# Lookahead of the weight pipeline in a fused transformer block: sums, casts and residues queued five, four and three units ahead, and the last pass begun with a pair

## The chip, the cores and the metric

The kernel runs on one core of one Trainium2 chip. The metric is device time in microseconds: the median of the runs of a kernel. The kernel before took 1093.7 us (three runs, 1092.52 to 1096.44). One execution more was taken with the hardware profiler; all views of the trace come from it.

## The reference

One layer of a hybrid block on x of 256 tokens by 2048 channels, in float32. The change touches only the last line of it, the SwiGLU part (D = 2048, hidden width 5632).

```python
xn = rms_norm(x, norm1_g)
q, k, v, ga, gg = split(xn @ w_in)          # 2048 -> 5120
att  = differential attention of 4 heads with RoPE, block-causal
u    = conformer convolution of ga * sigmoid(gg)
h    = x + concat(att, u) @ w_out           # 2048 -> 2048
hn   = rms_norm(h, norm2_g)
y    = h + (silu(hn @ w_gate) * (hn @ w_up)) @ w_down   # 2048 -> 5632 -> 2048
```

## The kernel before

**Arithmetic.** Each float32 operand is used as a rounded part (hi, type fp32r) and a residue (lo). A product is three matmuls: hi by hi, lo by hi, hi by lo. So each weight tile that is loaded must be cast on ACT (hi) and its residue must be made before TensorE (PE) can finish with it. The residue is made in one of two ways: DVE subtracts hi from the raw tile, or ACT writes the negated raw tile into lo and the POOL queue starts a DMA that adds the rounded weight's source on top (`by_dma`; these units have capital letters in the orders below).

**Units.** The program is a list of chunks, and PE takes them in this order. The early stages (w_in, w_out, and the first hidden block of gate and up, j = 0) use plain chunks. After that come "units" of two kinds:
- a *two* (letters g, G, u, U): 512 KB of weights, one tile `raw`, hi in `whi`, residue in `wlo`, 12 matmuls.
- a *pair* (letter s): 1 MB of weights in `wb`, on which one step of a Strassen-like scheme with seven products is done. DVE first makes four sums of the weights in `wt` (L963 to L965, three instructions), ACT casts the weights (L966) and the sums (L967) into `wh`, and DVE makes the residues `wl` of both (L971, L972). PE then does 21 matmuls (L988 to L990): for each of the seven products two with `wh` and one with `wl`. The first three products use columns of `wl` that L972 writes.

The stages of units are: gate and up blocks j = 1 to 3, then two passes of w_down (called d0.0 and d0.1), blocks 4 to 7, passes d1.0 and d1.1, blocks 8 to 10, passes d2.0 and d2.1. A block has 4 pairs and 8 twos in the order `sgGsgGsUUsUu` (`gugusgsUsGsU` for j = 1). The passes of w_down have 3 pairs and 10 twos, in the last group 3 pairs and 6 twos. A block needs 180 matmuls, a pass 183, a pass of the last group 135.

**End of a block.** After the last pair of a block DVE folds seven of the eight PSUM banks of products (`bank_sums`, L1086 to L1092), ACT applies SiLU (L1098), after the last unit DVE makes the hidden values (L1106, L1108, called u operations below), PE transposes them (L862) and ACT and DVE make hi and lo forms for w_down (`transposed`, `pair_forms`). These steps are Python generators: each `yield` is one resume, and `resume()` is called four times in a pair and twice in a two, so where a step is queued depends on how many resumes it has waited (`lag`). Passes of w_down add to the output by DMA. For j = 0 the hidden values are made at L829 (`up_done`).

**What sets the order of the work.** Each engine runs its own queue strictly in the order in which the program emits instructions; the order across engines is set by semaphores alone. `run_chunks` (L400) writes the queues: before it emits unit t to PE, it emits loads until unit t+5 (SP queue), casts of `by_dma` units until t+5 (ACT and POOL), the other casts until t+3, and residues until t+2. The sums of a pair are a part of its cast step (`round_pair`, L956), so they too are queued three units ahead. The buffers: 4 of `raw`, 4 of `whi`, 4 of `wlo`, 2 each of `wb`, `wh` and `wl`, 1 of `wt`. A load waits for the tile that it overwrites, whatever its place in the queue.

Of the kernel before, what the change touches and what calls it, by code (L numbers as in the profile page):

```python
# [12 lines left out]
F32 = mybir.dt.float32  # L13
F32R = mybir.dt.float32r
# [4 lines left out]
P = 128  # L19
# [12 lines left out]
N = 512  # L32
# [20 lines left out]
XPARTS = (range(0, 2), range(2, 4), range(4, 8), range(8, 12), range(12, 16))  # L53
# [3 lines left out]
AHEAD = 2  # L57
RAW_BUFS = 4
# [10 lines left out]
FGROUPS = (4, 4, 3)  # L69
# [12 lines left out]

PRODUCTS = ((Q6, 5, 1), (Q7, 6, 2), (Q5, 4, 3), (Q1, 0, 5), (Q2, 1, 6), (Q4, 2, 0), (Q3, 3, 4))

DOWN = (dict(pairs=((1, 0), (1, 1), (2, 0)), order="gsGgsGgsuUuUu"),
        dict(pairs=((4, 0), (4, 1), (5, 0)), order="gsGgsGgsuUuUu"),
        dict(pairs=((8, 0), (8, 1), (9, 0)), order="gsGsgsuUu"))

LOAD_AHEAD, DMA_AHEAD, HI_AHEAD, LO_AHEAD = 5, 5, 3, 2


BLOCKS = 2 * KD + 1
# [1 line left out]
TO_TRANSPOSE = 5  # L94
# [13 lines left out]
def tile_block(  # L108
# [6 lines left out]
    act, dve, pool, pe, sp = nc.scalar, nc.vector, nc.gpsimd, nc.tensor, nc.sync  # L115
# [174 lines left out]
    chunks = []  # L290
# [106 lines left out]
        if c["done"]:  # L397
            start(c["done"](ps))

    def run_chunks():  # L400
        n = len(chunks)
        loaded = split = 0
        rounded = [0, 0]

        def load(i):
            if i in before:
                before[i]()
            chunks[i]["load"](chunks[i])

        def do_round(which, until):  # L410
            while rounded[which] < min(n, until):
                c = chunks[rounded[which]]
                if c["by_dma"] == bool(which):
                    c["round"](c)
                rounded[which] += 1

        for t in range(n):
            load_lead, dma_lead, hi_lead, lo_lead = lead(t)
            while split < min(rounded[0], t + 1 + lo_lead):
                chunks[split]["split"](chunks[split])  # L420
                split += 1
            while loaded < min(n, t + 1 + load_lead):
                load(loaded)
                loaded += 1
                if load_lead == lo_lead:
                    do_round(1, loaded)
                    do_round(0, loaded)
                    chunks[split]["split"](chunks[split])
                    split += 1
            do_round(1, t + 1 + dma_lead)  # L430
            do_round(0, t + 1 + hi_lead)
            while split < min(n, t + 1 + lo_lead):
                chunks[split]["split"](chunks[split])
                split += 1
            chunks[t]["multiply"](chunks[t])
            if chunks[t].get("prompt") and chunks[t]["done"]:
                resume()
        while running:
            resume()
# [373 lines left out]
    ffn = {}  # L813
# [18 lines left out]
        yield from transposed(j, aa)  # L832

    def group_of(j):
        return next(g for g in range(len(FGROUPS)) if j < sum(FGROUPS[: g + 1]))

    def place(g):

        pairs = DOWN[g]["pairs"]
        at = 7 * len(pairs)  # L840
# [10 lines left out]
    def transposed(j, aa):  # L851
        g = group_of(j)
        if g not in down:
            place(g)
        d = down[g]
        for t in range(N // P // 2):
            pool_, tag = (aux_ps, "aux") if j else (acc_ps, "acc")
            pt = pool_.tile([P, 2, S], F32, tag=tag, name="ps_a")
            for i in range(2):
                for m in range(NM):  # L860
                    c = (2 * t + i) * P
                    pe.transpose(pt[:, i, m * P : (m + 1) * P], aa[m][:, c : c + P], ident)  # L862
            if (j, t) in d["pairs"]:
                yield from pair_forms(j, t, pt)
            else:
                hi, lo = d["at"][j, t]
                act.copy(hi, pt)
                yield from lag(2)
                dve.tensor_tensor(lo, pt, hi.bitcast(F32), ALU.subtract)  # L869
            d["ready"].add((j, t))  # L870
            yield from lag(2 if j else 1)

    def pair_forms(j, t, pt):

        fp = ffn["pool"]
        q = down[group_of(j)]["pairs"].index((j, t))
        fhi, flo = (f[:, :, q] for f in down[group_of(j)]["forms"])
        a = fp.tile([P, 2, NM, P], F32, tag="sum0", name="af")
        act.copy(a, pt)
        a11, a21, a12, a22 = a[:, 0, 0], a[:, 0, 1], a[:, 1, 0], a[:, 1, 1]  # L880
        act.copy(fhi[:, :2], a[:, :, 0])
        act.activation(fhi[:, 2], a22, AF.Copy, scale=-1.0)
        yield
        f = fp.tile([P, 4, P], F32, tag="sum2" if j else "sum1", name="fs")
        dve.scalar_tensor_tensor(f[:, 1], a21, -1.0, a22, ALU.mult, ALU.subtract)
        dve.scalar_tensor_tensor(f[:, 2], f[:, 1], -1.0, a11, ALU.mult, ALU.subtract)
        dve.tensor_tensor(f[:, 3], a11, a21, ALU.subtract)
        dve.tensor_tensor(f[:, 0], a12, f[:, 2], ALU.subtract)
        act.copy(fhi[:, 3:], f)
        yield  # L890
        dve.tensor_tensor(flo[:, :2], a[:, :, 0], fhi[:, :2].bitcast(F32), ALU.subtract)
        dve.scalar_tensor_tensor(flo[:, 2], a22, -1.0, fhi[:, 2].bitcast(F32), ALU.mult, ALU.subtract)
        yield
        dve.tensor_tensor(flo[:, 3:], f, fhi[:, 3:].bitcast(F32), ALU.subtract)

    forms = {}
# [56 lines left out]
        src = weights([(w, k, col, N) for w, col in c["sides"] for k in c["ks"]])  # L953
        sp.dma_start(out=c["b"].rearrange("p k n -> p (k n)"), in_=src)

    def round_pair(c):  # L956

        fp = ffn["pool"]
        assert "hi" in forms
        b = c["b"]  # L960
        c["t"] = t = fp.tile([P, 4, N], F32, tag="wt", name="wt")
        c["hi"] = fp.tile([P, 7, N], F32R, tag="wh", name="wh", bufs=2)
        dve.tensor_tensor(t[:, 2:4], b[:, 1:3], b[:, 0:1].to_broadcast([P, 2, N]), ALU.subtract)  # L963
        dve.tensor_tensor(t[:, 1], b[:, 1], t[:, 3], ALU.add)  # L964
        dve.tensor_tensor(t[:, 0], t[:, 1], b[:, 3], ALU.subtract)  # L965
        act.copy(c["hi"][:, 4:], b[:, 1:])  # L966
        act.copy(c["hi"][:, :4], t)  # L967

    def split_pair(c):
        c["lo"] = ffn["pool"].tile([P, 7, N], F32R, tag="wl", name="wl", bufs=2)  # L970
# [94 lines left out]
    def down_block(g, n):  # L1065

        last = g == len(FGROUPS) - 1 and n == D // N - 2
        ks = lambda jt: (jt[0] * (N // P) + 2 * jt[1], jt[0] * (N // P) + 2 * jt[1] + 1)
        pairs = DOWN[g]["pairs"]
        twos = [(j, t) for j in range(sum(FGROUPS[:g]), sum(FGROUPS[: g + 1])) for t in range(2) if (j, t) not in pairs]  # L1070
        units = fast_block(DOWN[g]["order"], ("w_down", n * N), ("w_down", (n + 1) * N),
                           [(q, ks(jt)) for q, jt in enumerate(pairs)], [(jt, ks(jt)) for jt in twos],
                           ready=lambda c: g in down and (pairs[c["p"]] if c["kind"] == "s" else c["p"]) in down[g]["ready"],
                           forms=lambda: down[g]["forms"],
                           plain=lambda c: [tuple(t[:, i, :] for t in down[g]["at"][c["p"]]) for i in range(2)])
# [25 lines left out]
    def block_done(j, q):  # L1101
        while "g" not in halfway:
            yield
        g, u = halfway.pop("g"), halfway.pop("u")
        for m, i in enumerate((Q3, QX)):
            dve.tensor_tensor(u[m], q[i], u[m], ALU.add)  # L1106
        for m in range(NM):
            dve.tensor_tensor(u[m], u[m], g[m], ALU.mult)  # L1108
        yield from lag(TO_TRANSPOSE)
        yield from transposed(j, u)  # L1110

    def add_to_out(m, n, t):
# [58 lines left out]
    for g, nb in enumerate(FGROUPS):  # L1171
# [7 lines left out]
        for n in range(0, D // N, 2):  # L1179
            down_block(g, n)  # L1180
        j0 += nb

    lead = lambda t: ((1,) * 4 if t < len(XPARTS) else (LOAD_AHEAD, DMA_AHEAD, HI_AHEAD, LO_AHEAD)
                      if "kind" in chunks[t] else (AHEAD,) * 4)
    for c, part in enumerate(XPARTS):
        before[c] = lambda part=part: x_load(part)
    before[0] = lambda: (x_load(XPARTS[0]), gain_columns(), x_part(XPARTS[0]), warm_up(WARM[1]), start(x_rest()))
    before[len(XPARTS)] = lambda: start(late_constants())
    run_chunks()


# [32 lines left out]
```

## Time and profile before

| | |
|---|---|
| runs, median (lowest to highest) | 1093.7 us (1092.52 to 1096.44) |
| profiled execution, its time | 1095.98 us |
| its span, first to last instruction | 1094.2 us |
| mean granted TensorE clock | 0.988 |
| DVE, ACT, POOL busy | 902.5, 654.9, 130.5 us |

The views are read like this. The page gives the busy time of each engine over the span. The view of waits lists who waited for whom: the waiting engine with the tile and the line, the releaser, then microseconds in total, how many times, and the longest. The view by windows gives, for each stretch, its length, then busy time (and number of instructions) of PE, of the weight loads PEld, of DVE, ACT and POOL, then the granted clock, the share of the DMA engines and GB/s. The timeline gives start and duration of each instruction, and in square brackets the idle time of the engine before it with what ended it. L and a number is a line of the kernel before.

### The profile page before, as it was taken

What the parts mean: (1) busy time and instruction counts of PE and PEld (TensorE: products, weight loads), DVE (VectorE), ACT (ScalarE), POOL (GpSimd) and SP (SyncE); (2) the same over time, 40 slices, a digit from 0 to 9 for tenths busy, and PEclk for the clock granted to TensorE, in tenths of its full rate; (3) what the DMA queues carried; (4) which work ended last, traced back from release to release, by engine and by line L of the source; (5) the groups of instructions that cost most, each with busy time, mean ns of one, the idle gap of its engine ahead of it and who ended that gap; (6) DMA issues with size and microseconds to landing.
All of it is one profiled execution on the core that took longest, in us unless ns stands there. A gap on an engine that the chain in (4) does not pass through costs nothing.

```text
span 1094.2 us, 13181 instructions
## 1 busy us (share of the span) xinstructions
PE 1051.0 (96%) x4780; PEld 865.5 (79%) x4780; DVE 902.5 (82%) x1124; ACT 654.9 (60%) x831; POOL 130.5 (12%) x176
## 2 busy tenths in 40 slices
PE   8999999999999999989999999899999999899698
PEld 7988888877888877777878888778878888687586
DVE  4799989898755788888878878889796888897877
ACT  6544566755754656657556566576665475766432
POOL 0120112201000000101011211010101110001011
PEclk9999999999999999999999999999999999999899
DMA  8556555444467469798779997978969998888564
GB/s 295 196 183 201 191 175 174 154 154 154 135 212 241 163 232 292 216 277 211 235 227 280 304 316 211 266 208 255 303 172 295 291 280 282 223 260 229 198 180 102
DMA packets 62445, 245.47 MB, mean 224 GB/s; under 512 B 6964, under 2 KB 8430, under 8 KB 54956
## 3 DMA queue, kind: packets, MB, share of 16 engines
q1 hardware_dynamic: 48576, 200.56, 51.6%
q0 software_dynamic: 13744, 44.05, 22.0%
q8 instruction: 37, 0.61, 0.2%
q14 instruction: 28, 0.23, 0.1%
q10 hardware_dynamic: 60, 0.03, 0.0%
HBM read 236.22 MB, written 8.39 MB: 224 GB/s over the span
## 4 chain that ended last, share of the span: by engine, by line
PE 34%; DVE 16%; ACT 8%; issue 6%; DMA 2%; POOL 0%; SPq 0%; DVEq 0%; ACTq 0%
PE q L1007 7%; PE q L1006 7%; PE q L1011 6%; PE q L990 5%; PE q L988 5%; PE q L989 5%; DVE wl L972 4%; ACT wh L967 3%; DMA raw<-in_wts_dram 2%; DVE wt L963 2%; ACT whi L333 2%; DVE wlo L342 2%; ACT wlo L336 2%; DVE wl L971 1%; DVE wt L964 1%
## 5 line engine op out<-in xcount | busy, mean ns | idle before, releaser
L333 ACT CAST whi<-raw 128x1024 fp32r<-128x1024 f32 (+1 forms) x261 | 268.8, 1047 | 134.6 <-DMA raw<-in_wts_dram 54.7
L342 DVE TENSOR_TENSOR wlo<-raw,whi 128x1024 fp32r<-128x1024 f32 (+1 forms) x193 | 233.4, 1218 | 74.6 <-ACT whi L333 74.4
L372 PE MATMUL acc<-whi,lhi 128*128 128x512 f32 (+1 forms) x448 | 168.3, 380 | 3.2 <-ACT lhi L239 2.9
L967 ACT CAST wh<-wt 128x2048 fp32r<-128x2048 f32 x58 | 110.8, 1910 | 99.3 <-DVE wt L965 99.1
L373 PE MATMUL acc<-whi,llo 128*128 128x512 f32 (+1 forms) x448 | 166.5, 376 | 0.5 <-DVE llo L240 0.4
L972 DVE TENSOR_TENSOR wl<-wt,wh 128x2048 fp32r<-128x2048 f32 x58 | 132.9, 2291 | 10.4 <-ACT wh L967 9.6
L990 PE MATMUL q<-wl,fhi 128*128 128x512 f32 x280 | 112.8, 403 | 17.6 <-DVE wl L972 17.6
L337 POOL DMA_DIRECT2D wlo<-in_wts_dram x68 | 61.4, 903 | 553.1 <-ACT wlo L336 468.1
L1006 PE MATMUL q<-whi,chi 128*128 128x512 f32 x320 | 124.7, 390 | 0.0
L1007 PE MATMUL q<-whi,clo 128*128 128x512 f32 x320 | 124.6, 389 | 0.0
L971 DVE TENSOR_TENSOR wl<-wb,wh 128x1536 fp32r<-128x1536 f32 x58 | 101.7, 1753 | 22.2 <-ACT wh L966 22.2
L378 PE MATMUL acc<-wlo,lhi 128*128 128x512 f32 (+1 forms) x448 | 114.4, 380 | 1.7 <-DVE wlo L342 1.7
L988 PE MATMUL q<-wh,fhi 128*128 128x512 f32 x280 | 112.4, 401 | 2.5 <-DVE llo L869 2.4
L989 PE MATMUL q<-wh,flo 128*128 128x512 f32 x280 | 111.5, 398 | 0.0
L526 DVE SCALAR_TENSOR_TENSOR y<-upad,cw,y 128x256 f32<-128x256 f32 x240 | 103.8, 483 | 4.4 <-ACT y L519 3.9
L372 PEld LDWEIGHTS acc<-whi,lhi 128*128 128x128 f32 x448 | 84.9, 189 | 18.9 <-ACT lhi L239 3.3
L373 PEld LDWEIGHTS acc<-whi,llo 128*128 128x128 f32 x448 | 84.9, 190 | 15.7 <-DVE llo L240 0.9
L378 PEld LDWEIGHTS acc<-wlo,lhi 128*128 128x128 f32 x448 | 79.6, 188 | 17.3 <-DVE wlo L342 3.0
L966 ACT CAST wh<-wb 128x1536 fp32r<-128x1536 f32 x58 | 85.1, 1468 | 3.9 <-issue 2.5
L1011 PE MATMUL q<-wlo,chi 128*128 128x512 f32 x320 | 86.4, 392 | 0.0
L990 PEld LDWEIGHTS q<-wl,fhi 128*128 128x128 f32 x280 | 53.9, 192 | 32.6 <-DVE wl L972 21.0
L336 ACT ACTIVATE wlo<-raw 128x1024 fp32r<-128x1024 f32 x68 | 71.7, 1054 | 0.0
(213 smaller groups left out, 1717.6 us busy)
## 6 DMA issues: line engine op xcount, KB each, us to landing
raw<-in_wts_dram SPq DMA_DIRECT2D x259, 512.0 KB, 4.9
wb<-in_wts_dram SPq DMA_DIRECT2D x58, 1024.0 KB, 6.7
wlo<-in_wts_dram POOLq DMA_DIRECT2D x68, 512.0 KB, 8.1
out_dram<-sum POOLq DMA_DIRECT2D x22, 256.0 KB, 7.4
out_dram<-h POOLq DMA_DIRECT2D x8, 256.0 KB, 5.7
h<-in_x_dram SPq DMA_DIRECT2D x6, 256.0 KB, 8.1
h<-in_x_dram SPq DMA_DIRECT2D x4, 128.0 KB, 3.4
raw<-in_wts_dram SPq DMA_DIRECT2D x2, 256.0 KB, 4.3
```

The source lines that it names most:

```text
L333: act.copy(c["hi"], c["raw"])
L342: dve.tensor_tensor(c["lo"], c["raw"], c["hi"].bitcast(F32), ALU.subtract)
L372: pe.matmul(ps[m], xhi[:, ms], hi[:, j, :], start=c["first"] and j == 0, stop=False)
L373: pe.matmul(ps[m], xlo[:, ms], hi[:, j, :], start=False, stop=False)
L378: pe.matmul(ps[m], xhi[:, ms], lo[:, j, :], start=False, stop=c["last"] and j == nk - 1)
L972: dve.tensor_tensor(c["lo"][:, :4], c["t"], c["hi"][:, :4].bitcast(F32), ALU.subtract)
L988: pe.matmul(ps, fhi[:, f, p, :], c["hi"][:, w], start=bool(first), stop=False)
L989: pe.matmul(ps, flo[:, f, p, :], c["hi"][:, w], start=False, stop=False)
L990: pe.matmul(ps, fhi[:, f, p, :], c["lo"][:, w], start=False, stop=bool(last))
L1006: pe.matmul(ps, plain[i][0][:, ms], hi[:, i, :], start=i == 0 and bool(c["first"].get(qs[m])), stop=False)
L1007: pe.matmul(ps, plain[i][1][:, ms], hi[:, i, :], start=False, stop=False)
L1011: pe.matmul(sum_bank(c, qs[m]), plain[i][0][:, ms], lo[:, i, :], start=False, stop=i == 1 and bool(c["last"].get(qs[m])))
```

## The change

The order of the queues for the units is rewritten. The core of the diff:

```diff
-DOWN = (dict(pairs=((1, 0), (1, 1), (2, 0)), order="gsGgsGgsuUuUu"),
-        dict(pairs=((4, 0), (4, 1), (5, 0)), order="gsGgsGgsuUuUu"),
-        dict(pairs=((8, 0), (8, 1), (9, 0)), order="gsGsgsuUu"))
-
-LOAD_AHEAD, DMA_AHEAD, HI_AHEAD, LO_AHEAD = 5, 5, 3, 2
+DOWN = (dict(pairs=((1, 0), (1, 1), (2, 0)), order=("gsGgsGgsuUuUu",) * 2),
+        dict(pairs=((4, 0), (4, 1), (5, 0)), order=("gsGgsGgsuUuUu",) * 2),
+        dict(pairs=((8, 0), (8, 1), (9, 0)), order=("sgsGgsuUu",) * 2))
+
+LOAD_AHEAD, DMA_AHEAD, SUMS_AHEAD, HI_AHEAD, LO_AHEAD = 9, 5, 5, 4, 3
...
+    def may_load(i):
+        c = chunks[i]
+        if "kind" not in c:
+            return False
+        if "sides" in c:
+            o = earlier(pair_at, i, 2)
+            return "hi" in forms and (o is None or o in parted)
+        o = earlier(two_at, i, RAW_BUFS)
+        return o is None or o in parted or (o in rounded and chunks[o]["by_dma"])
...
+    def may_sum(i):
+        o = earlier(pair_at, i, 1)
+        return "sides" not in chunks[i] or (loaded[0] > i and (o is None or o in parted))
...
         for t in range(n):
...
+            if t >= first - AHEAD:
+                until("part", part_of, t + 1 + LO_AHEAD)
+                until("sums", sums_of, t + 1 + SUMS_AHEAD, may=may_sum)
+                until("dma", round_of, t + 1 + DMA_AHEAD, lambda c: c["by_dma"])
+                until("round", round_of, t + 1 + HI_AHEAD)
+                load_until(t + 1 + LOAD_AHEAD)
+            else:
+                until("part", part_of, t + 1 + (1 if t < len(XPARTS) else AHEAD))
+            part_of(t)
             chunks[t]["multiply"](chunks[t])
...
@@ def transposed
-                yield from lag(2)
+                yield from lag(3 if j else 2)
@@ def pair_forms, twice
-        yield
+        yield from lag(2)
...
-    def round_pair(c):
+    def pair_sums(c):
         b = c["b"]
-        c["t"] = t = fp.tile([P, 4, N], F32, tag="wt", name="wt")
+        c["t"] = t = ffn["pool"].tile([P, 4, N], F32, tag="wt", name="wt")
         dve.tensor_tensor(t[:, 2:4], b[:, 1:3], b[:, 0:1].to_broadcast([P, 2, N]), ALU.subtract)
         dve.tensor_tensor(t[:, 1], b[:, 1], t[:, 3], ALU.add)
         dve.tensor_tensor(t[:, 0], t[:, 1], b[:, 3], ALU.subtract)
-        act.copy(c["hi"][:, 4:], b[:, 1:])
-        act.copy(c["hi"][:, :4], t)
+
+    def round_pair(c):
+        c["hi"] = ffn["pool"].tile([P, 7, N], F32R, tag="wh", name="wh", bufs=2)
+        act.copy(c["hi"][:, 4:], c["b"][:, 1:])
+        act.copy(c["hi"][:, :4], c["t"])
...
@@ def block_done
-        yield from lag(TO_TRANSPOSE)
+        yield from lag(TO_TRANSPOSE if group_of(j) == group_of(j + 1) else 3)
```

So residues go from two to three units ahead, casts from three to four, and the sums of a pair, now a step of their own, from three to five, as soon as the pair is loaded and the residues of the pair before it are queued. Loads are queued up to nine units ahead as soon as the instruction that frees their tile is queued. The new rule starts two chunks before the first unit, where the old one kept two chunks of lead. Both passes of the last group begin with a pair instead of a two. After the last block of a group the transposes are queued after three resumes instead of five; the lo forms of a transposed tile come one resume later, the second and third step of the pair forms one each. No instruction is added to or taken from any engine; the number of buffers is the same.

More of the change, by code (lines that the diff above doesn't have):

```diff
@@ L1 @@
+import bisect
 import math
@@ L398, in multiply, with earlier, load_until @@
             start(c["done"](ps))
[L400 to L405, printed above, removed]
+    loaded, rounded, parted = [0], set(), set()
+    pair_at, two_at = [], []
+    def earlier(at, i, n):
+        k = bisect.bisect_left(at, i) - n
+        return at[k] if k >= 0 else None
+    def may_load(i):
[7 more added lines that the diff above has]
+        return o is None or o in parted or (o in rounded and chunks[o]["by_dma"])
+    def load_until(n, forced=False):
+        while loaded[0] < min(n, len(chunks)):
+            i = loaded[0]
+            if not (forced or may_load(i)):
+                return
+            loaded[0] += 1
             if i in before:
@@ L408, in load @@
             chunks[i]["load"](chunks[i])
[L410 to L415, printed above, removed]
-        for t in range(n):
[L418 to L434, printed above, removed]
+    def may_sum(i):
+        o = earlier(pair_at, i, 1)
+        return "sides" not in chunks[i] or (loaded[0] > i and (o is None or o in parted))
@@ new lines, in sums_of, with round_of, part_of @@
+    def sums_of(i):
+        c = chunks[i]
+        if "sides" in c and "t" not in c:
+            load_until(i + 1, True)
+            o = earlier(pair_at, i, 1)
+            if o is not None:
+                part_of(o)
+            pair_sums(c)
+    def round_of(i):
+        if i not in rounded:
+            rounded.add(i)
+            load_until(i + 1, True)
+            sums_of(i)
+            chunks[i]["round"](chunks[i])
+    def part_of(i):
+        if i not in parted:
+            parted.add(i)
+            round_of(i)
+            chunks[i]["split"](chunks[i])
@@ new lines, in run_chunks, with until @@
+    def run_chunks():
+        n = len(chunks)
+        pair_at.extend(i for i, c in enumerate(chunks) if "sides" in c)
+        two_at.extend(i for i, c in enumerate(chunks) if "kind" in c and "sides" not in c)
+        at = dict(part=0, dma=0, sums=0, round=0)
+        first = next(i for i, c in enumerate(chunks) if "kind" in c)
+        def until(what, do, stop, only=lambda c: True, may=lambda i: True):
+            while at[what] < min(n, stop) and may(at[what]):
+                if only(chunks[at[what]]):
+                    do(at[what])
+                at[what] += 1
+        for t in range(n):
+            if t >= first - AHEAD:
[7 more added lines that the diff above has]
+            part_of(t)
@@ L834, in group_of @@
     def group_of(j):
-        return next(g for g in range(len(FGROUPS)) if j < sum(FGROUPS[: g + 1]))
+        return next((g for g in range(len(FGROUPS)) if j < sum(FGROUPS[: g + 1])), None)
     def place(g):
@@ L889, in pair_forms @@
         act.copy(fhi[:, 3:], f)
-        yield
+        yield from lag(2)
         dve.tensor_tensor(flo[:, :2], a[:, :, 0], fhi[:, :2].bitcast(F32), ALU.subtract)
@@ L954, in load_pair @@
         sp.dma_start(out=c["b"].rearrange("p k n -> p (k n)"), in_=src)
-    def round_pair(c):
-        fp = ffn["pool"]
+    def pair_sums(c):
         assert "hi" in forms
         b = c["b"]
-        c["t"] = t = fp.tile([P, 4, N], F32, tag="wt", name="wt")
-        c["hi"] = fp.tile([P, 7, N], F32R, tag="wh", name="wh", bufs=2)
+        c["t"] = t = ffn["pool"].tile([P, 4, N], F32, tag="wt", name="wt")
         dve.tensor_tensor(t[:, 2:4], b[:, 1:3], b[:, 0:1].to_broadcast([P, 2, N]), ALU.subtract)
@@ L1070, in down_block @@
         twos = [(j, t) for j in range(sum(FGROUPS[:g]), sum(FGROUPS[: g + 1])) for t in range(2) if (j, t) not in pairs]
-        units = fast_block(DOWN[g]["order"], ("w_down", n * N), ("w_down", (n + 1) * N),
+        units = fast_block(DOWN[g]["order"][n // 2], ("w_down", n * N), ("w_down", (n + 1) * N),
                            [(q, ks(jt)) for q, jt in enumerate(pairs)], [(jt, ks(jt)) for jt in twos],
@@ L1181, in tile_block @@
         j0 += nb
-    lead = lambda t: ((1,) * 4 if t < len(XPARTS) else (LOAD_AHEAD, DMA_AHEAD, HI_AHEAD, LO_AHEAD)
-                      if "kind" in chunks[t] else (AHEAD,) * 4)
     for c, part in enumerate(XPARTS):
```

## Prediction

> **What bounds the kernel now.** I read the page first, then the waits of PE, then the windows stage by stage.
>
> ```profile
> PE 1051.0 (96%) x4780; PEld 865.5 (79%) x4780; DVE 902.5 (82%) x1124; ACT 654.9 (60%) x831; POOL 130.5 (12%) x176
> PE q L990 <- DVE wl L972: 18.6, 11, 3.5
> PE q L1007 <- DVE llo L869: 4.4, 1, 4.4
> PE q L1006 <- ACT lhi L867: 3.3, 1, 3.3
> PE q L988 <- DVE llo L869: 2.4, 1, 2.4
> PE ps_a L862 <- DVE alo L869: 2.3, 2, 1.2
> ```
>
> PE is the bound, and what it waits for is residues: eleven times those of a pair (L972), and four times a form of the hidden values. Nothing here waits for a load. The windows below run from the first matmul of a stage of units to that of the next (starts from the timeline of PE), in this order: blocks 1, 2, 3, passes d0.0, d0.1, blocks 5, 6, 7, pass d1.0, blocks 9, 10, passes d2.0, d2.1.
>
> ```profile
> 399.07:445.16 46.09, 43.66 (x190) 35.63 (x188) 41.13 (x36) 28.80 (x24) 3.54 (x4) 0.96 0.89 297
> 445.16:492.45 47.29, 42.65 (x189) 34.34 (x188) 42.28 (x53) 30.25 (x32) 4.30 (x5) 1.00 0.81 242
> 492.45:538.53 46.08, 43.71 (x189) 35.64 (x188) 37.52 (x43) 30.29 (x31) 4.34 (x5) 0.96 0.79 218
> 538.53:582.39 43.86, 42.67 (x192) 35.05 (x191) 34.86 (x35) 23.57 (x22) 5.23 (x6) 1.00 0.83 246
> 582.39:623.90 41.51, 41.51 (x185) 34.27 (x183) 35.21 (x33) 26.79 (x24) 7.02 (x8) 1.00 1.00 285
> 664.70:710.78 46.08, 42.39 (x190) 34.41 (x188) 40.86 (x50) 30.05 (x31) 4.30 (x5) 1.00 0.81 231
> 710.78:757.11 46.33, 43.67 (x189) 35.56 (x188) 40.80 (x45) 30.61 (x31) 4.32 (x5) 0.96 0.83 247
> 757.11:798.88 41.77, 41.77 (x190) 34.57 (x188) 34.68 (x35) 27.82 (x26) 4.33 (x5) 1.00 0.84 240
> 798.88:842.64 43.76, 42.65 (x193) 35.06 (x191) 34.77 (x35) 23.47 (x22) 5.21 (x6) 1.00 0.84 247
> 924.96:972.22 47.26, 43.75 (x190) 35.58 (x188) 42.33 (x51) 31.96 (x34) 4.32 (x5) 0.96 0.80 234
> 972.22:1015.09 42.87, 42.06 (x189) 34.49 (x188) 34.95 (x41) 27.64 (x28) 4.35 (x5) 1.00 0.77 209
> 1015.09:1058.15 43.06, 34.83 (x144) 27.63 (x143) 33.40 (x33) 18.60 (x18) 3.47 (x4) 0.88 0.63 183
> 1058.15:1090.05 31.90, 31.39 (x136) 24.92 (x134) 26.80 (x28) 12.04 (x10) 5.14 (x6) 1.00 0.59 149
> ```
>
> Block 7 and pass d0.1 are undisturbed (PE busy throughout at full clock): 41.77 us for 180 matmuls and eight transposes, 41.51 us for 183 matmuls, so 0.227 us a matmul and 41.77 - 180 x 0.227 = 0.9 us for the transposes. A pass with eight transposes should take 42.4, one of the last group 135 x 0.227 = 30.6, with transposes 31.5. What each stage took beyond that is what any schedule could win: block 1 4.3, block 2 5.5, block 3 4.3, d0.0 1.4, blocks 5 and 6 4.3 and 4.6, d1.0 1.3, blocks 9 and 10 5.5 and 1.1, d2.0 11.5, d2.1 1.3. The sum is 45.1 us, about 31 of it waits and the rest the granted clock (0.96 and 0.88) after them. The early stages aren't touched by the change. Something within 0.5% (5.5 us) can't be told from no change here.
>
> **Why the third pair of a block is late.** The timeline of DVE, then of ACT, in block 5:
>
> ```profile
> 681.24 0.69 DVE L965 TENSOR_TENSOR wt<-wt,wb 128x512 f32<-128x512 f32 x1
> 685.21 0.29 DVE L885 SCALAR_TENSOR_TENSOR fs<-af 128x128 f32<-128x128 f32 x1 [3.28 <-ACT af L879]
> 686.69 1.75 DVE L971 TENSOR_TENSOR wl<-wb,wh 128x1536 fp32r<-128x1536 f32 x1
> 688.36 2.28 DVE L972 TENSOR_TENSOR wl<-wt,wh 128x2048 fp32r<-128x2048 f32 x1
> ```
> ```profile
> 682.80 1.91 ACT L967 CAST wh<-wt 128x2048 fp32r<-128x2048 f32 x1
> 684.61 0.58 ACT L879 COPY af<-ps_a 128x512 f32<-128x512 f32 x1
> ACT wh L967 <- DVE wt L965: 99.1, 35, 6.8
> ```
>
> DVE ends the sums at 681.9, stands 3.3 us before the pair forms of block 4, which ACT has queued behind the cast of this pair, and makes the residues only then. Sums, cast and residue of one pair follow each other with no slack, two or three units before PE needs them; ACT waited for such sums 35 times.
>
> **Residues, casts and sums a unit or two earlier.** At the start of a block the new DVE queue reads: sums of the second pair, bank_sums, u operations, residue of the second pair, sums of the third, first pair forms, residue of the third. Counted from the first matmul of the block: bank_sums (4.65 us, rows below) can start when PE ends the last pair, 5.4 us before; the u operations must wait for zero and take 2.56; residue 1.75 + 2.28, a two's residue 1.22, sums 1.22 + 0.69 + 0.69, forms about 1, and the residue of the third pair ends about 16 to 17 us, while PE reaches that pair after 2 x 4.76 + 4 x 2.72 + 0.5 = 21 us. The margin is 4 us where today it is -3.5, and the cast no longer waits for the sums. So I take the pair waits of blocks 2, 3, 5, 6, 9, 10 and d2.1 away, with the clock behind them. What is late next is DVE itself: 40.86 us of work in block 5 against 41.77 of PE. Margins of 1 us will be cut now and then; I leave 1.5 us for all of them. The ends: 0, and half of today's 26.6 us in these stages.
>
> ```profile
> 1010.37 0.68 DVE L1086 COPY sum<-q 128x512 f32<-128x512 f32 x1
> 1014.34 0.68 DVE L1092 TENSOR_TENSOR sum<-q,sum 128x512 f32<-128x512 f32 x1
> 1020.01 1.28 DVE L1108 TENSOR_TENSOR sum<-sum,sum 128x512 f32<-128x512 f32 x2
> ```
>
> **Starts of the passes.** With three resumes the transposes of the last block are queued 18 matmuls (4.1 us) into the pass. In d0.0 and d1.0 DVE has bank_sums, 2.60 of sums and 2.56 of u operations (two groups like L1108) until then and is done at about 5 us: a wait of about 1 us each, in place of 1.4 and 1.3. In d2.0 a pair's residue lies before the u operations: 1015.02 + 4.03 + 2.56 = 1021.6 against 1019.2, a wait of 2.4 plus about 1 of clock. The forms of block 10 then have two pairs and a two of PE's time before the first unit that needs them, so the two waits of 3.3 and 4.4 us of today go. d2.0 loses 3.4 instead of 11.5.
>
> **Block 1 gets worse.** Here the new rule starts before the first unit, and the sums of the first pair come into the DVE queue ahead of a two's residue and ahead of L829, the hidden values of block 0.
>
> ```profile
> 399.51 1.22 DVE L342 TENSOR_TENSOR wlo<-raw,whi 128x1024 fp32r<-128x1024 f32 x1 [0.41 <-ACT whi L333]
> 400.65 1.40 DVE L829 SCALAR_TENSOR_TENSOR a<-acc,rstd,sil 128x512 f32<-128x512 f32 x2
> 402.31 1.48 ACT L966 CAST wh<-wb 128x1536 fp32r<-128x1536 f32 x1 [1.35 <-DMA wb<-in_wts_dram]
> 403.61 0.60 PE L862 MATMUL ps_a<-ident,a 128*128 128x128 f32 x4
> 415.55 0.50 PE L988 MATMUL q<-wh,fhi 128*128 128x512 f32 x1 [2.43 <-DVE llo L869]
> ```
>
> The weights of that pair land at 402.3, and the order of loads and what frees their tiles up to there stay as they are. So DVE, free at 400.7, waits until 402.3, makes the sums (404.9), the residue of the two (406.1) and L829 (407.5). PE wants the transposes at 403.6: a new wait of 3.9 us. Then L869 of block 0, for whose PSUM bank PE waits today 2.43 us in the fourth product of the first pair: DVE has before it residue (4.03), sums (2.60), two's residue (1.22), L869 (0.69), residue of the second pair (4.03), sums of the third (2.60), and itself: 407.5 + 15.9 = 423.4. PE, 3.9 us later than today, is there at 413.1 + 3.9 = 417.0. A wait of about 6 us (the instructions overlap by some tenths). With the clock, 1.9 us today (4.3 less 2.43), block 1 loses 3.9 + 6 + 1.9 = 11.8 in place of 4.3. The ends: 4.3 if the sums wait for nothing, and 13.7 with a second loss of clock.
>
> [...]
>
> **Loads.** The queue of SP keeps its order, and it waits for tiles already, not for its place:
>
> ```profile
> SPq L954 <- DVE wl L971: 327.0, 47, 17.5
> ACT whi L333 <- PE q L1007: 48.1, 18, 6.4
> DMA to landing us min/median/max: 5.2/8.1/11.8
> ```
>
> So nine instead of five is worth nothing by itself; loads start earlier only by as much as the residues free tiles earlier. DMA has the room: share 1.00 in d0.1 with no loss.
>
> **The sum.** 45.1 less what stays (11.8 block 1, 2.0 for d0.0 and d1.0, 3.4 for d2.0, 1.5 others) is 26.4 us. The profiled execution took 1095.98 (span 1094.2), so it would be 1069.6; against the median of the runs, 2.3 lower, 1067.3. I predict 1067.
>
> **Rivals.**
> - *Block 1 doesn't pay* (0.12): the sums wait for no load, or the other waits leave less than I think. Block 1 at 4.3 or below and the rest as above: 1060 to 1054. Against it: the 1.35 us that ACT waits for that very load.
> - *The casts run into their four buffers* (0.12). In the five twos at the end of a pass the cast four units ahead needs a fifth `whi`, so ACT stands until PE is done, with the next pass's pair cast behind it (row L333: 48.1 us of such waits today, where they harm nobody). After 1.8 of the third of these twos ACT needs 1.05 + 1.05 for the two in front, 1.48 + 1.91 for the pair, DVE 2.28: 7.8 us against 9.1 of PE, a margin of 1.3. If the ring makes it wait for the next unit the margin is -1.4; with clock 3 us in four passes: 1079.
> - *Slower* (0.05): DVE comes late to bank_sums. More of its work for coming pairs is queued before them, and the next block's first products need those banks. It decides from 3.8 us late on (5.2 of lead less the 1.4 of two folds). Late by a pair's sums and residue (6.6), each of 15 starts would lose 2.8 and up to 1.9 of clock, 42 to 70 us, against 33 saved: 1102 to 1131. Against it: 40.86 of 41.77 is the fullest block, most have 35.
> - *Accumulates get late, no change* (0.04). A residue made by DMA is started 5 units (13.6 us) before PE's unit, and its second half comes 1.8 us later; less 2.1 on ACT and 0.9 on POOL it may land in 12.4 us. Today's slowest takes 11.8. If more loads in flight made the typical 8.1 into 13, half of the 68 such units would lose 0.6 to 0.8: 1067 + 24 = 1091. [...]
>
> **How the numbers follow.** The forecast has 0.67, 1060 to 1074. The range takes in the first two rivals: 1056 to 1080. Faster by over 0.5%: forecast, first and second rival, 0.91, less a little for worse mixtures: 0.89. Within: 0.06. Slower: 0.05.
>
> **What would show it.** Right: PE's wait for L972 falls from 18.6 to under 4 us; ACT's wait for L965 from 99 to under 30; the windows of blocks 2, 3, 5, 6, 9 come to 42 to 43 us; d2.0 to about 35; PE stands at L862 in block 1 for about 4 us with L829 late, then about 6 us at L988 for L869; block 1 takes 53 to 54. Wrong: pair waits that only move to another pair; new waits of PE for `wlo` landed by DMA or for bank_sums; a short block 1.

## The result and the profile after

The changed kernel takes 1076.5 us (median of four runs, 1075.8 to 1077.3) against 1093.4 for the kernel before in the same series: ratio 0.984, 95% interval 0.982 to 0.986. Run again beside the later experiments it took 1075.1 (ratio 0.981, 0.980 to 0.983). So it is faster by 17 to 20 us, where 26.4 were forecast. The profiled execution took 1075.79 us (span 1074.0).

The lines have new numbers: the residues L971 and L972 are now L1015 and L1016, the sums' last L965 is L1006, the cast L967 is L1011, the transposes L862 are L905, the first matmul of a product L988 is L1032, the forms L867 and L869 are L910 and L912, the first pair form L885 is L928, block 0's hidden values L829 are L872, the folds L1086 to L1092 are L1130 to L1136, the u operations L1106 and L1108 are L1150 and L1152.

First the page's line of busy times, then the waits of PE (engine, tile and line, releaser, us in total, times, longest):

```profile
PE 1044.6 (97%) x4780; PEld 861.5 (80%) x4780; DVE 900.4 (84%) x1124; ACT 654.0 (61%) x831; POOL 129.9 (12%) x176
```
```profile
PE ps_a L905 <- DVE a L872: 4.7, 2, 4.4
PE q L1032 <- DVE llo L912: 4.5, 1, 4.5
PE ps_a L905 <- DVE sum L1152: 4.2, 6, 2.5
...
PE q L1032 <- DVE sum L1130: 1.7, 2, 1.3
...
PE q L1050 <- DVE sum L1135: 1.2, 2, 0.6
...
PE q L1032 <- DVE sum L1134: 0.7, 2, 0.4
```

The waits for the residues of pairs, 18.6 us before, are gone altogether. In their place stand waits for steps of the hidden values: L872, L912, L1152 and the folds (the last three rows, 3.6 us in all).

The windows of the stages (length, PE, PEld, DVE, ACT, POOL busy, granted clock, DMA share, GB/s): blocks 1, 2, 3, pass d0.0, d0.1; blocks 5, 6; block 9; pass d2.0.

```profile
397.04:453.15 56.11, 46.59 (x189) 37.28 (x188) 43.93 (x39) 30.99 (x26) 3.55 (x4) 0.91 0.78 245
453.15:497.16 44.01, 42.39 (x188) 34.31 (x189) 40.09 (x49) 28.08 (x30) 4.31 (x5) 1.00 0.83 248
497.16:540.48 43.32, 42.36 (x189) 34.31 (x189) 39.53 (x45) 28.83 (x29) 4.35 (x5) 1.00 0.89 275
540.48:584.27 43.79, 43.05 (x192) 35.08 (x192) 33.71 (x35) 26.52 (x26) 5.24 (x6) 1.00 0.74 213
584.27:625.75 41.48, 41.48 (x185) 34.35 (x183) 35.76 (x34) 23.91 (x20) 7.04 (x8) 1.00 0.98 278
...
666.55:708.32 41.77, 41.77 (x190) 34.58 (x189) 37.45 (x44) 29.94 (x31) 4.31 (x5) 1.00 0.83 246
708.32:750.43 42.11, 42.09 (x190) 34.49 (x188) 40.62 (x46) 28.83 (x28) 4.33 (x5) 1.00 0.90 277
...
919.03:960.79 41.76, 41.76 (x189) 34.58 (x188) 37.09 (x43) 29.39 (x31) 4.32 (x5) 1.00 0.83 242
...
1002.85:1039.19 36.34, 33.59 (x144) 27.22 (x143) 34.52 (x35) 20.80 (x19) 3.52 (x4) 0.95 0.66 201
```

Blocks 5 and 9 now take the undisturbed 41.77 us. Block 1 has become the worst stage: 56.11 us, where it was 46.09. Some of DVE's operations at the start of block 1 and PE's two long waits there (timelines; start, duration, and in brackets the idle time before):

```profile
401.57 1.23 DVE L1004 TENSOR_TENSOR wt<-wb 128x1024 f32<-128x1024 f32 x1 [2.73 <-DMA wb<-in_wts_dram]
...
405.30 1.40 DVE L872 SCALAR_TENSOR_TENSOR a<-acc,rstd,sil 128x512 f32<-128x512 f32 x2
...
421.52 0.68 DVE L912 TENSOR_TENSOR llo<-ps_a,lhi 128x512 fp32r<-128x512 f32 x1
```
```profile
406.10 0.33 PE L905 MATMUL ps_a<-ident,a 128*128 128x128 f32 x1 [4.36 <-DVE a L872]
...
422.25 0.79 PE L1032 MATMUL q<-wh,fhi 128*128 128x512 f32 x1 [4.45 <-DVE llo L912]
```

DVE stands 2.73 us for the load of the first pair with L872 queued behind the sums, as the prediction read it; PE then stands 4.36 us, and later 4.45 us for L912, which is behind two pairs' residues and sums.

### The profile page after: what moved, and what is told of

Read it like the earlier page. It is cut to its first block, busy times and chain, and to the rows that moved or that the text cites. A ratio compares the mean times of both kernels' runs of the same rounds, so it can differ in the third digit from the quotient of the medians.

```text
span 1074.0 us, 13249 instructions
## 1 busy us (share of the span) xinstructions
PE 1044.6 (97%) x4780; PEld 861.5 (80%) x4780; DVE 900.4 (84%) x1124; ACT 654.0 (61%) x831; POOL 129.9 (12%) x176
## 4 chain that ended last, share of the span: by engine, by line
PE 55%; DVE 7%; issue 2%; ACT 1%; DMA 1%; DVEq 0%; SPq 0%; ACTq 0%
PE q L1050 10%; PE q L1051 10%; PE q L1055 10%; PE q L1032 8%; PE q L1033 8%; PE q L1034 8%; DVE wl L1016 1%; DVE wlo L343 1%; PE ps_a L905 1%; DVE wt L1004 1%; DMA wb<-in_wts_dram 1%; DVE wt L1005 0%; ACT whi L334 0%; DVE wl L1015 0%; ACT wh L1011 0%
## 5 line engine op out<-in xcount | busy, mean ns | idle before, releaser
L1015 DVE TENSOR_TENSOR wl<-wb,wh 128x1536 fp32r<-128x1536 f32 x58 | 101.7, 1753 | 42.5 <-ACT wh L1010 42.5
L1016 DVE TENSOR_TENSOR wl<-wt,wh 128x2048 fp32r<-128x2048 f32 x58 | 132.7, 2287 | 1.0
L1011 ACT CAST wh<-wt 128x2048 fp32r<-128x2048 f32 x58 | 110.8, 1910 | 35.3 <-DVE wt L1006 35.0
L1032 PE MATMUL q<-wh,fhi 128*128 128x512 f32 x280 | 110.8, 396 | 6.8 <-DVE llo L912 4.5
L1034 PE MATMUL q<-wl,fhi 128*128 128x512 f32 x280 | 109.9, 392 | 0.0
L1004 DVE TENSOR_TENSOR wt<-wb 128x1024 f32<-128x1024 f32 x58 | 70.8, 1221 | 4.2 <-DMA wb<-in_wts_dram 3.6
L337 ACT ACTIVATE wlo<-raw 128x1024 fp32r<-128x1024 f32 x68 | 71.8, 1056 | 0.2 <-PE q L1055 0.2
```

The lines of the kernel that those rows point to most:

```text
L1016: dve.tensor_tensor(c["lo"][:, :4], c["t"], c["hi"][:, :4].bitcast(F32), ALU.subtract)
L1032: pe.matmul(ps, fhi[:, f, p, :], c["hi"][:, w], start=bool(first), stop=False)
L1034: pe.matmul(ps, fhi[:, f, p, :], c["lo"][:, w], start=False, stop=bool(last))
```

## The experiments

All are the changed kernel with one or two edits. The table puts their results together. A loss is the time of a stage (from its first matmul to that of the next, by PE's timeline; the last pass to the end of its last unit) beyond the undisturbed length given in the prediction (40.8 us for blocks 4 and 8, which begin without transposes). A wait in front of a stage's first matmul is thus counted to the stage before it. The losses come from one profiled execution of each kernel, the ratios from four to ten runs. "Leads" are the units by which sums, casts and residues are ahead.

| kernel | leads | block 1 | blocks 2 to 10 | d0.0, d1.0 | last group | sum | ratio to before (95%) |
|---|---|---|---|---|---|---|---|
| before | 3/3/2 | 4.3 | 25.3 | 2.7 | 12.7 | 45.0 | 1 |
| changed | 5/4/3 | 14.3 | 5.1 | 2.6 | 4.8 | 26.8 | 0.984 (0.982 to 0.986) |
| changed, again | 5/4/3 | 13.2 | 4.9 | 2.6 | 4.8 | 25.5 | 0.981 (0.980 to 0.983) |
| e1 hold block 1's start | 5/4/3 | 4.9 | 6.1 | 2.6 | 5.9 | 19.5 | 0.974 (0.972 to 0.976) |
| e5 five resumes | 5/4/3 | 12.3 | 5.2 | 1.0 | 3.8 | 22.3 | 0.979 (0.977 to 0.981) |
| e6 old last order | 5/4/3 | 11.9 | 9.1 | 2.6 | 7.3 | 30.9 | 0.990 (0.986 to 0.993) |
| e3 sums alone ahead | 5/3/2 | 7.7 | 31.8 | 7.8 | 2.4 | 49.7 | 1.003 (1.002 to 1.005) |
| e4 sums at four | 4/4/3 | 8.7 | 3.0 | 1.8 | 6.0 | 19.5 | 0.974 (0.973 to 0.976) |
| e10 residues at two | 5/4/2 | 8.2 | 5.7 | 6.2 | 1.0 | 21.1 | 0.979 (0.977 to 0.982) |
| e9 sums four, residues two | 4/4/2 | 7.6 | 1.7 | 0.0 | 0.1 | 9.4 | 0.969 (0.966 to 0.971) |
| e12 all at three | 3/3/3 | 10.0 | 9.5 | 2.0 | 10.7 | 32.2 | 0.985 (0.982 to 0.989) |
| e13 old leads | 3/3/2 | 4.0 | 4.8 | 7.1 | 2.9 | 18.8 | 0.975 (0.971 to 0.979) |
| e8 hold, sums four | 4/4/3 | 4.9 | 3.2 | 1.8 | 6.3 | 16.2 | 0.973 (0.971 to 0.974) |
| e11 hold, residues two | 4/4/2 | 2.5 | 3.8 | 0.0 | 0.0 | 6.3 | 0.964 (0.962 to 0.966) |

**First group: what did the new leads do?** My theory was that residues and casts a unit earlier take the pair waits away, and that block 1 pays for sums queued ahead of its hidden values. The rival: the sums' own lead is what pays.

e1 lets the new rule begin with the first unit and not two chunks before it. For the first four units of block 1 it keeps residues at two units and sums and casts at three, in the fourth at two:

```diff
-            if t >= first - AHEAD:
+            if first <= t < first + 4:
+                near = 2 if t == first + 3 else 3
+                until("part", part_of, t + 1 + AHEAD)
+                until("sums", sums_of, t + 1 + near, may=may_sum)
+                until("dma", round_of, t + 1 + DMA_AHEAD, lambda c: c["by_dma"])
+                until("round", round_of, t + 1 + near)
+                load_until(t + 1 + LOAD_AHEAD)
+            elif t >= first:
```

> The new leads begin only four units into block 1; until then residues two and sums and casts three units ahead (two in the fourth unit), so that the hidden values of block 0 (L829 of before) and their low forms (L869 of before) are queued ahead of the sums of the first and the residue of the second pair. Theory (what is queued before them on DVE costs block 1): PE's waits of 4.4 us for the hidden values and 4.5 us for the low form go, and with them both losses of clock; block 1 takes 42 to 45 us instead of 56.1, the kernel 1063 to 1066. Rival (the loads that the new rule queues earlier crowd the DMA engines there, whose share is 1.0 from 396 to 404 us, and the first pair's weights are late for anything): block 1 stays above 52 us and the kernel at 1073 or more.

It took 1068.4 us, and block 1 lost 4.9 us in place of 14.3; neither of its two long waits is left. So the new start of block 1 is a loss by itself, and nearly all of it comes from the place of the first pairs' steps. Less was won than I expected, since another wait came forward. In the waits of PE of e1 (its lines from L470 on stand seven further down, so L1137 is the first fold):

```profile
PE q L1039 <- DVE sum L1137: 4.4, 3, 3.7
PE ps_a L912 <- DVE sum L1159: 4.0, 5, 2.5
```

Before the first matmul of block 2 PE stood 3.7 us for the first fold of block 1, which was queued behind sums and residue of the coming pairs. This wait makes up most of the 4.9.

e3 and e4 each leave one half of the new leads:

```diff
-LOAD_AHEAD, DMA_AHEAD, SUMS_AHEAD, HI_AHEAD, LO_AHEAD = 9, 5, 5, 4, 3
+LOAD_AHEAD, DMA_AHEAD, SUMS_AHEAD, HI_AHEAD, LO_AHEAD = 9, 5, 5, 3, 2   (e3)
+LOAD_AHEAD, DMA_AHEAD, SUMS_AHEAD, HI_AHEAD, LO_AHEAD = 9, 5, 4, 4, 3   (e4)
```

> After with the casts back at three and the residues at two units ahead; only the sums stay five ahead. Theory (the lead of the residue is what PE sees; sums alone help because the cast no longer waits for them, but DVE still meets the forms of the block before ahead of the residue of the third pair): waits of PE for pair residues of 4 to 12 us in all come back in blocks 2, 3, 5, 6, 9, each 1 to 3 us longer than in after; 1080 to 1086, less what block 1 may win. Rival (taking the sums out of the cast step is the whole gain): the blocks stay as in after, no wait for L1016 of more than 1 us in all, 1074 to 1077.

> After with the sums queued four units ahead, directly before the cast that reads them; casts four, residues three ahead. Theory (the lead of the residue is what PE sees): ACT waits for the sums again, 35 us become 60 to 100, but PE hardly waits for pair residues, blocks 5 and 9 stay under 43 us and the kernel is at 1075 to 1079. Rival (the detached sums are the gain): waits of PE for L1016 of 8 us or more come back, 1084 or more.

With the sums alone further ahead (e3, 1099.9 us) the gain is gone, and 0.3% more than that; both of my ranges were too low, by 14 us and more. The waits of PE of e3 show the mechanism that the prediction named as its slower rival, work for coming pairs ahead of the folds:

```profile
PE q L1034 <- DVE wl L1016: 10.6, 9, 1.2
PE q L1032 <- DVE sum L1130: 9.4, 6, 3.2
PE ps_a L905 <- DVE sum L1152: 4.8, 6, 1.6
```

With the sums together with the casts (e4, 1068.3, below both of my ranges) the kernel is faster than the changed one by 0.7 to 1.0%: the sums' fifth unit costs. From this I took it that the leads of casts and residues are the gain; e13 below shows that this was wrong.

e5 gives the transposes after the last block of a group five resumes again:

```diff
-        yield from lag(TO_TRANSPOSE if group_of(j) == group_of(j + 1) else 3)
+        yield from lag(TO_TRANSPOSE)
```

> After with the transposes behind the last block of a group queued after five resumes again, as before, instead of three. Theory (PE comes to these transposes ahead of DVE's u operations): the six waits of 4.2 us in all at L905 for L1152 go; d0.0 and d1.0 take 42.6 to 43 instead of 43.8 us, d2.0 32 to 33 instead of 36.3; the kernel gains 4 to 6 us, 1070 to 1072.5. Rival (the forms then come too late for the first unit that needs them): the wait moves to the low and high forms of block 10 in d2.0, which takes 36 us or more; the kernel is at 1075 or more.

It took 1073.5. The starts of d0.0 and d1.0 lost 0.5 us each instead of 1.3, as expected; d2.0 lost 3.8 instead of 4.8, less than hoped for. Its interval overlaps that of the changed kernel's second series, so only the stages tell the two apart.

**Second group.** The changed kernel ran again here, so that the rest can be read beside it:

> The changed kernel once more, beside the kernels of this group. Its first ratio was 0.984, so beside a kernel before at 1096.2 about 1078.7 us; no theory says otherwise. It is here so that the differences of the other kernels are read on one chip.

It took 1075.1 us, 3.6 below that estimate; its ratio's interval overlaps the first one.

e6 has the old order in the last group, `gsGsgsuUu`.

> The changed kernel with the last group's old order (each of its passes begins with a two, pairs in second, fourth and sixth place). Theory A: the first pair in front hides the pair forms of block 10, and without it the two waits of 3.3 and 4.4 us that the kernel before had at that place come back in part: pass d2.0 loses 8 to 11 us instead of 4.8, time 1082 to 1085. Rival B: the longer lead already makes the forms early (no pair's casts stand in front of them), and the order is worth nothing: d2.0 loses 4 to 6 us, time 1078 to 1080.

It took 1083.5 us, 8.4 more than the changed kernel beside it. These stand first among the waits of PE:

```profile
PE q L1032 <- DVE llo L912: 6.0, 1, 6.0
PE q L1050 <- DVE sum L1135: 5.1, 3, 3.9
PE q L1050 <- ACT lhi L910: 3.7, 1, 3.7
```

The first is block 1's (4.5 in the changed kernel's profile). The others stand mainly at the start of d2.0: by PE's timeline 3.86 us for a fold before its first unit, and 3.66 for the form `lhi` at its third. So the pair in front is worth some 6 to 7 us by the stages (4.3 + 7.3 against 0.3 + 4.8 in block 10 and d2.0). It hides the forms, as expected, and a fold too, which I had not seen.

e8 is e1 and e4 together.

> Sums four units ahead (with the casts), casts four, residues three, and the first four units of block 1 held at the old leads. Theory A: the early sums and the start of block 1 are two separate losses, so the savings add. Block 1 loses 2 to 4 us (8.7 with sums at four alone, 4.9 with the hold alone), the wait for the folds of block 1 at the start of block 2 (3.7 us with the hold alone) falls under 1; the sum of losses is 10 to 13 us, time 1060 to 1064. Rival B: both cure the same DVE queue in block 1, and the two together are no better than either: block 1 loses 4.5 to 5.5, time 1067 to 1069.

It took 1065.4 us, below the range of the rival and above that of my theory. Block 1 lost 4.9 as with the hold alone, and the wait for the first fold stayed:

```profile
PE q L1039 <- DVE sum L1137: 3.7, 1, 3.7
```

e9 has the residues two units ahead, sums and casts four:

```diff
+LOAD_AHEAD, DMA_AHEAD, SUMS_AHEAD, HI_AHEAD, LO_AHEAD = 9, 5, 4, 4, 2
```

> Sums and casts four units ahead, residues two ahead as in the kernel before. Theory A: what pays is that DVE is given the residue a unit earlier, ahead of the forms and sums that would hold it; casts ahead alone leave the residue at its old place. PE again waits for residues of pairs, 8 to 18 us over all, time 1085 to 1095. Rival B: the residue was late only because its cast waited for fresh sums on ACT; with the cast a unit earlier the residue is free to run at once, waits of PE for residues of pairs are under 4 us, and the time is 1066 to 1072.

It took 1060.0 us: my theory missed by 25 us, and the rival did better than it promised. A window each of blocks 3 and 5 and passes d0.0 and d2.0 in e9:

```profile
490.35:532.11 41.76, 41.76 (x189) 34.56 (x188) 37.38 (x42) 30.13 (x30) 4.35 (x5) 1.00 0.85 244
532.11:574.56 42.45, 42.45 (x193) 35.13 (x191) 34.66 (x35) 24.04 (x22) 5.24 (x6) 1.00 0.80 243
656.84:698.61 41.77, 41.77 (x190) 34.57 (x189) 39.52 (x48) 29.83 (x31) 4.31 (x5) 1.00 0.88 258
...
990.40:1022.09 31.69, 31.69 (x144) 26.05 (x143) 30.59 (x31) 17.28 (x16) 3.49 (x4) 1.00 0.67 181
```

From block 3 on the stages lose some 0.3 us in all. The residue's third unit of lead is a cost (e4 against e9: 1068.3 against 1060.0); by the order of the queue it puts 4 us of residue ahead of folds and u operations.

**Third group.** e10 is the changed kernel with residues at two (5/4/2), e12 has all three at three, and e13 has the old leads (3/3/2) with everything else of the change.

> The changed kernel (sums five, casts four) with residues at two units ahead again. Theory A (what pays is the cast a unit ahead of its residue; sums at five and residues at three each put work in front of the steps of the hidden values, and each costs on its own): the losses lie between the 26 us of the changed kernel and the 9 us of sums and casts at four; sums at five cost here what they cost beside residues at three, 7 to 10 us, time 1066 to 1071. Rival B (only the two together fill DVE's queue; with residues at two, sums at five do no harm): 1058 to 1062. Rival C (residues at three were what paid beside sums at five): 1090 or more.

> Sums, casts and residues all three units ahead: only the residues are earlier than in the kernel before. Theory A: with no unit between cast and residue the chain of sums, cast and residue has no slack again, ACT stands for fresh sums (75 us or more) and DVE then for the cast; PE waits for residues of pairs or for folds, time 1078 to 1095. Rival B: a residue a unit earlier is enough by itself, 1064 to 1072.

> The changed kernel with the old leads: sums and casts three units ahead, residues two. What is left of the change is the last group's order, the later forms, the three resumes, the new start of the units and the loads up to nine. Theory A: the cast a unit earlier is what takes PE's waits for residues of pairs away; without it they are back (10 us or more at the third matmul of the products), blocks 2, 3, 5, 6, 9 lose 3 to 6 us each, and only the last pass gains, by 5 to 8 us: time 1086 to 1093. Rival B: the later forms (a resume more) alone let DVE through to the residue, and the leads are worth only the rest: waits for residues of pairs under 5 us, time 1070 to 1080.

e10 took 1072.2, just above my range: sums at five cost 12 us beside residues at two (against e9) and 7 to 8 beside residues at three (the changed kernel against e4). e12 took 1079.6, within my range, but PE waited for a form and for u operations more than for residues of pairs:

```profile
PE q L1032 <- DVE llo L912: 6.5, 1, 6.5
PE ps_a L905 <- DVE sum L1152: 5.5, 1, 5.5
...
PE q L1034 <- DVE wl L1016: 3.1, 3, 1.1
```

e13 took 1067.7 us (ratio 0.975), 18 us below what my theory gave and 2 below the rival, which put the gain on the later forms. With none of the new leads the change wins more than with them. Its waits, first PE's, then ACT's:

```profile
PE q L1034 <- DVE wl L1016: 3.7, 5, 1.0
PE ps_a L905 <- DVE sum L1152: 2.7, 6, 0.6
```
```profile
ACT wh L1011 <- DVE wt L1006: 86.8, 36, 5.9
```

ACT still stands 86.8 us for fresh sums (99.1 before), so that wait was not what hurt PE. And beside these leads sums at five alone cost 32 us (e3 against e13). The timeline of DVE in block 5 of e13, at the third pair, shows what did:

```profile
673.74 0.68 DVE L937 TENSOR_TENSOR llo<-fs,lhi 128x512 fp32r<-128x512 f32 x1
674.65 1.76 DVE L1015 TENSOR_TENSOR wl<-wb,wh 128x1536 fp32r<-128x1536 f32 x1 [0.24 <-ACT wh L1010]
676.47 2.29 DVE L1016 TENSOR_TENSOR wl<-wt,wh 128x2048 fp32r<-128x2048 f32 x1
678.67 0.29 DVE L928 SCALAR_TENSOR_TENSOR fs<-af 128x128 f32<-128x128 f32 x1
```

Before, the second set of pair forms (L885, 685.21) came ahead of this pair's residue (686.69) and made DVE stand 3.28 us. Here the residue goes first and stands for 0.24 us. The waits of DVE for forms in the kernel before:

```profile
DVE llo L869 <- ACT lhi L867: 14.5, 5, 3.3
DVE fs L885 <- ACT af L879: 9.8, 3, 3.3
```

The three for L885 are in blocks 2, 5 and 9. In blocks 3, 6 and 10 it was the single form `llo` (L869) that stood 3.3 us ahead of the third pair's residue. In e13 DVE waits for neither of the two (but 4.9 us for `alo`, another form made by the line of `llo`). Up to the second half of block 10 the queues of DVE and of ACT in e13 have the same instructions as before and differ only in where the forms stand, those of the pairs and the single ones. So in blocks 2 to 9 it is the later forms (`lag(2)` and `lag(3)`) that took the pair waits away. What e13 lacks, sums and casts four ahead give (e9, 1060.0): the starts of d0.0 and d1.0, where e13 loses 7.1 us, and the kernel before lost 2.7.

e11 joins e9 with the hold of e1, with one line more, so that the sums of the second pair of block 2 come after the folds of block 1:

```diff
-            if first <= t < first + 4:
+            if first <= t < first + 4 or t == first + 11:
```

> Sums and casts four units ahead, residues two, and the first four units and the last unit of block 1 held at the old lead of three for sums and casts. Theory A: the three waits left in the units (2.0 us for the hidden values of block 0, 1.4 for their residue, 3.3 for the folds of block 1) come from sums queued ahead of them; block 1 loses 1 to 3 us instead of 7.6, block 2 under 1 instead of 1.7, time 1052 to 1056. Rival B: the waits come back at the second or third pair of block 1, as in the kernel before (block 1 loses 4.3 or more): 1056 to 1060.

It took 1056.8 us, ratio 0.964, the best of all: 38.5 us below the kernel before in its series, 18.3 below the changed one. By its time it lies in the rival's range, 0.8 us above mine. Block 1 lost 2.5 us, as mine said; block 2, at 2.2, more than I gave it, with a wait of 1 us for a pair's residue as in e13.

Loads at six instead of nine were not timed. With that edit to the changed kernel the program emits the same instructions in the same order on all five engines: a load waits for its tile to be freed before it can be queued further ahead.

## Why the prediction was right, and where not

**The sum.** The stage losses were to fall from 45.1 to 18.7 us; they fell to 26.8. The other 2 us of the profiled executions' difference of 20.2 lie ahead of the units (block 1 starts at 397.04, before at 399.07), in stages that the change leaves alone; in the other kernels block 1 starts between 396.8 and 398.6. The medians differ by 17.0, less than the profiles, because the profiled execution of before lay 2.5 us above its median and that of after 0.7 below. The 1076.5 us lie above the 1060 to 1074 that the forecast gave its own case. They lie within 1056 to 1080 only because that range took in the rival of the casts, which did not come about; that they fall within it is in part luck. The 8.1 us too much are 3.6 in "others", 2.5 in block 1, 1.4 in d2.0 and 0.6 in d0.0 and d1.0.

**Block 1** is the largest term, and it was put too small: a loss of 11.8 us was forecast and 14.3 measured, 10 more than before. The mechanism was the one described. The waits were 4.4 and 4.45 where 3.9 and 6 stood in the sum. The clock was put at 1.9 us and cost about 5 (56.11 us at 0.91; after the second wait it was 0.58 from 424 to 428 us).

**The starts of the passes.** About 1 us each was forecast for d0.0 and d1.0, 1.3 each came. For d2.0 a wait of 2.4 at the transposes was forecast, and 2.47 is in its timeline. But the stage lost 4.8 instead of 3.4, mainly because the clock fell to 0.95, about 1.8 us of 36.34, where 1 us was allowed. The two waits of 3.3 and 4.4 us for the forms of block 10 are gone, as forecast.

**Others.** For all other places 1.5 us were left; it was 5.1. Blocks 2 and 3 lost 3.8 of them, mainly through folds queued behind sums of coming pairs. That is the slower rival's mechanism on a small scale, and waits for folds were among the prediction's signs of being wrong; the prediction held the mechanism for all or nothing and gave it no share in the sum. ACT's wait for sums fell from 99.1 to 35.0 us, where under 30 was named as a sign of being right.

**Residues, casts and sums a unit or two earlier: the step that failed.** "I take the pair waits of blocks 2, 3, 5, 6, 9, 10 and d2.1 away" came true, but the leads to which it was credited were not needed for it. The prediction quoted the very row that held the residue up, DVE standing 3.28 us at L885. It gave the move of the forms, which is part of the same change, no price, and it did not see the second such place, L869 in blocks 3, 6 and 10. e13 shows the waits nearly gone (18.6 to 3.7 us) without the new leads. The leads as the change sets them, against e13, cost about 0.6 to 0.9%: 10 us in block 1 and 2 in the last group, against 4.5 won at d0.0 and d1.0. The part of them that pays is the fourth unit of the casts, with the sums that they need (e9 against e13: 0.969 against 0.975, with intervals that just fail to meet). Sums at five take away more than that (e10 against e9: 0.979), residues at three about as much (e4 against e9: 0.974; e12 against e13: 0.985 against 0.975).

**The rivals.** That block 1 doesn't pay: refuted, it lost 14.3 us. Casts running into their four buffers: ACT's waits for them did grow,

```profile
ACT whi L334 <- PE q L1051: 59.2, 22, 6.4
```

from 48.1 before, but pass d0.1 still takes 41.48 us, so they harm nobody. Late accumulates: no wait of PE for `wlo` of a by_dma unit appears.

**Still open.** The later forms, the last group's order and the three resumes were not each put back into e13. For blocks 2 to 9 the queues settle it; in the last group, e6 prices the order only beside the new leads. No run has the new leads with the forms at their old places, so whether the leads alone would have taken the pair waits away is not known. And why e13 loses more at the starts of d0.0 and d1.0 than the kernel before (7.1 against 2.7 us) was not taken apart.

## What to carry to other kernels

On an engine that runs its queue in order, a step that is emitted earlier is also emitted ahead of something else. DVE ran so in block 5 of the kernel before: it stood until 685.21 for L885, and the residue behind that (L971) started at 686.69, though the casts that it reads had ended by 684.71. Price a longer lead by what it pushes back: here the folds, the u operations and the hidden values, which PE wants at once. When a wait is traced to an operation that stands in front of the late one in its queue, as L885 did, move that operation first. A longer lead for the late one can come after, one step at a time: here the fourth unit of casts (with their sums) paid, and the fifth of sums and the third of residues cost.

## What the runs showed of the hardware

In these traces the clock's loss after a wait does not go by the wait's length alone. Two windows of the kernel before, each 4 us long and begun about 1.5 us after the end of a wait of 3.5 us for the residue of a block's third pair (block 2, then block 9; the third last column is the granted clock):

```profile
474.00:478.00 4.00, 4.00 (x20) 3.30 (x19) 3.62 (x5) 2.46 (x2) 0.00 (x0) 1.00 0.99 278
952.00:956.00 4.00, 4.00 (x12) 3.10 (x12) 3.63 (x5) 2.34 (x2) 0.00 (x0) 0.59 1.00 283
```

The same wait cost nothing in one window and some 8 matmuls of 20 in the other, about 1.8 us. Over whole stages (the windows in the prediction) the third wait of 3.5 us, in block 5, left the clock at 1.00 too, while shorter ones, of 2.4 us in block 3 and 2.7 in block 6, went with 0.96. After the wait of 4.45 us in block 1 of the changed kernel the clock lay low until 428 us:

```profile
420.00:424.00 4.00, 1.75 (x4) 1.46 (x5) 2.13 (x4) 0.00 (x0) 0.00 (x0) 0.56 1.00 291
424.00:428.00 4.00, 4.00 (x12) 3.11 (x12) 0.00 (x0) 0.60 (x1) 0.00 (x0) 0.58 0.35 70
428.00:432.00 4.00, 4.00 (x20) 3.30 (x19) 3.04 (x2) 4.00 (x4) 0.00 (x0) 1.00 0.13 20
```
